# Sixteen experts' weights in tiles of whole rows, gate before up, and a moved combine and gather

## The chip, the cores and the metric

The kernel is one program on one core of one Trainium2 chip. It runs three transformer-like blocks over 512 tokens of 1024 channels, one after the other. The metric is the time on the device in microseconds (us). Three runs of the kernel before took 3489.10, 3494.49 and 3498.57 us; their median is 3494.49 us.

## The reference, cut to what matters

Only the mixture of experts at the end of the first block is touched by the change. There are 16 experts, and each takes the 64 tokens that score highest for it (capacity 2 * 512 / 16 = 64):

```
logits = h @ w_router;  aff = softmax(logits)            # h: 512 x 1024
top_w, top_idx = top_k(aff.T, 64)                        # 64 tokens for each of 16 experts
xe = h[top_idx]                                          # 16 x 64 x 1024
g  = xe @ w_gate[e];  u = xe @ w_up[e]                   # 1024 x 2048 each
y  = (silu(g) * u) @ w_down[e]                           # 2048 x 1024
out = zeros.at[top_idx].add(y * top_w)                   # back to the 512 tokens
```

All of it is float32. An expert has three matrices of 8.39 MB; the 16 experts have 402.7 MB, and every byte is read once from device memory.

## The kernel before, in words

`phase_m` holds the mixture of experts; `phase_a` runs before it, `phase_b` and `phase_c` (the other two blocks) after it. The experts are taken in pairs, p = 0 to 7, so that 2 x 64 tokens fill the 128 partitions.

For one pair the work has these parts. `gather(p)` (L2271) multiplies the tokens by a one-hot matrix on TensorE (L2277) and writes the pair's tokens `xe`, scaled and shifted, by ScalarE and VectorE (L2284, L2286). `expert(e, ...)` (L2318) does one expert. `weights(p)` (L2297) makes `gT`, which holds a token's weight for each slot; it multiplies on GpSimd (L2302) and transposes on TensorE (L2304). `combine(p, ...)` (L2357) multiplies the pair's results `yp` by `gT` (L2362) and adds them to the sums `acc` on VectorE (L2369).

In `expert`, the 2048 hidden columns are done in two halves, c = 0 and 1. Within a half, loads of gate and of up take turns: four tiles of each, and each tile holds two blocks of 128 rows by 1024 columns (`wexp`, L2309). A partition of a tile thus receives two separate pieces of 4096 bytes. Four matmuls use a tile, two for each block, whose outputs lie on the lower and the upper 64 partitions of one bank of PSUM (L2330). Then come silu on ScalarE (L2336), the product on VectorE (L2338) and four transposes (L2341) into `tp`, whose copy is `hTe`. After both halves eight tiles of down follow, 256 rows of 1024 columns each, again in two pieces of 4096 bytes to a partition, with four matmuls to a tile (L2352). Each expert therefore has 24 tiles of 1 MiB: eight of gate, eight of up, eight of down.

All weight loads are issued by SyncE (SP) in order, on one DMA queue. `wtile` (L284) hands out the room: the first 16 tiles have room of their own (12 in the rotation, four `wpre`); from then on a tile takes the room of the one 12 places before it, and its load waits until TensorE has used that. A tile's room may be called `w`, `wh` or `wx`; the names say nothing about the content.

The order on each engine is not the order of the Python text: a planner that works with estimated costs and priorities orders the whole program at build time, so that transposes, gather and combine can stand between the matmuls of an expert. `s.tc.issue_after(last.ins)` (L2332) only forces the last quarter of the first gather behind a given matmul.

In the text, `gather(p + 1)` and `weights(p)` stand between the two experts of a pair, and `combine(p)` stands after the second. The share of the last pair is added in `tiles()` (L2384), inside `phase_b`.

Of the kernel before, what the change touches and what calls it, by code (L numbers as in the profile page):

```python
# [19 lines left out]
P = 128  # L20
# [15 lines left out]
# name: (K, N, k tiles in a chunk, columns in a chunk)  # L36
# [33 lines left out]
# columns of a rotated head of 64 whose halves are 0..31 and 32..63, so that partners lie 16 apart  # L70
# [3 lines left out]
def _pair_cols(n_kv, rep):  # L74
    # heads (2g, r), (2g+1, r) side by side
    out = []
    for g in range(n_kv // 2):
        for r in range(rep):
            for s in range(2):
                h = (2 * g + s) * rep + r  # L80
                out.append(np.arange(64) + 64 * h)
    return np.concatenate(out)


def _tables_2d(n_meta):
    """cos and signed sin of the 2-d rotation, channel p of a head on partition p (64 twice)."""
# [12 lines left out]
def host(i):  # L99
    """Inputs of the program: layouts of the given arrays, and constants of the shapes."""  # L100
# [70 lines left out]
def _rwkv_masks():  # L171
    """[row in chunk (twice), direction, masks of 64 columns]: s before t; s up to t; for blocks of 1 to 32
    the diagonal and the rows of the later half of a pair against the columns of the earlier; the first of
    these transposed."""
# [38 lines left out]
class Kern:  # L213
# [24 lines left out]
    def a8(s, name, w=512):  # L238
        """Eight channel tiles."""
        q = [s.a4(f"{name}{i}", w) for i in range(2)]  # L240
        return [q[k // 4][:, k % 4] for k in range(8)]

    def parts(s, name, w=512):
        """Room for the two parts of eight channel tiles."""
# [9 lines left out]
    def split(s, x, h, l, scale=None):  # L254
        """x (times scale) as the sum of two float32r tiles h and l."""
# [9 lines left out]
    def stack(s, t, out, pr):  # L265
        """out: the parts of head pr of a pair of heads, h at the head's own rows, l at the other's."""
# [5 lines left out]
    def swap(s, a, b):  # L272
        """b: the halves of stack's a in the other order. a's product with a stack of another, plus b's, is exact."""
        for h in range(2):
            s.nc.gpsimd.dma_start(b[64 * h:64 * h + 64].bitcast(F32R), a[64 - 64 * h:128 - 64 * h].bitcast(F32R))

    def wsplit(s, name, ci, ki=0, into=None):
        """A chunk of weights as two float32r tiles whose sum it is."""
# [28 lines left out]
    def consts(s):  # L307
# [16 lines left out]
        # for a norm that follows another: the products of the gains, the squares of the first's  # L324
# [22 lines left out]
    def ssq(s, st, c0, tiles, nt, scale=None, first=True, last=True, ntok=P, add=None):  # L347
        """Column c0+n of st[tokens]: the sum over channels of squares of token tile n."""
# [5 lines left out]
    def sumsq(s, st, c0, x, nt, k, kt, first=True, last=True, ntok=P, add=None, **kw):  # L354
        """One of kt tiles of ssq: all but the last are first added up."""
# [15 lines left out]
    def twonorms(s, x, gains, xh, xl, lin, lead):  # L371
        """For a norm followed by a second one: the parts of x times both's gains, tile by tile, each followed by
        lead(k, parts); a psum tile whose columns 0..3 get the tokens' sums of squares of x, 4..7 those of x times
        the first norm's gains."""
# [24 lines left out]
    def factors(s, st, pool):  # L399
        """The tokens' factors of the first norm, 1 / sqrt(m), and of both, 1 / sqrt(m2 + eps m), of twonorms' sums."""  # L400
# [14 lines left out]
    def spread(s, r, nt, out, psum):  # L415
        """out[:, 128 n + t] = r[t, n] on every partition."""
# [10 lines left out]
    def lin(s, name, j, kt, x, ps, w=None, ntile=512):  # L427
        """ps = (x @ W[:, 128 j : 128 j + 128]).T of channel-major x."""
# [3 lines left out]
    def wcols(s, name, j0, nj):  # L432
        """Yields j, f for column tiles j0..j0+nj-1; f(k) is the k-th stationary tile."""
# [12 lines left out]
    def wcols3(s, name, j0, nj):  # L446
        """As wcols; f(k) is the pair of parts of the k-th stationary tile."""
# [10 lines left out]
    def cols(s, gen, x, lin):  # L458
        """Yields j, its product for the column tiles of wcols3."""
# [5 lines left out]
    def mm3(s, ps, a, b, first, last):  # L465
        """ps (+)= a.T @ b of pairs of parts."""
# [8 lines left out]
    def turns(*gens):  # L475
        """Takes the generators' stages by turns."""
# [10 lines left out]
    def heads_spread(s, r, n, psum):  # L487
        """psum[64 h + i, t] = r[t, h] for n tokens: r is [tokens, 2]."""
# [8 lines left out]
def phase_b(s, x2):  # L497
    nc, d = s.nc, s.d
    T2 = 528
    with ExitStack() as octx:  # L500
# [18 lines left out]
        # the meta tokens' keys, each head's among zeros, and the queries' scores against them  # L519
# [3 lines left out]
        # the meta tokens' keys, rates and running sums as a chunk padded with zeros  # L523
# [17 lines left out]
        # the meta tokens  # L541
# [75 lines left out]
        def normrot(t, W, g, out, sc):  # L617
            """Norm over each head's 64 channels, then rotation; W = 528 with the meta tokens first."""
# [93 lines left out]
        def load(n):  # L712
            """Loads of the recurrence's step n."""
# [38 lines left out]
def rwkv_prep(s, p1, lin, lin2, r4, k4, v4, wd, ad, bd2, bo_d, ch_d, v_d, mt):  # L752
    """Rates, keys and running sums of the decays' logarithms, by chunk in DRAM; the bonus."""
# [20 lines left out]
    # token-major v by chunk, the meta tokens last  # L774
# [12 lines left out]
    for t in range(4):  # L787
# [31 lines left out]
        # kk is kept negated  # L819
# [4 lines left out]
        # bonus  # L824
# [17 lines left out]
# direction, chunk, chunk of v: the meta tokens precede the forward chunks  # L842
# [3 lines left out]
def rwkv(s, ps, pr_, load, srcs, v_d, msk, y4, fill):  # L846
    """The recurrences over chunks of 64 tokens, both directions by turns. Two chunks are prepared at a time, stage
    by stage in turn with the chain of the chunk before them and a piece of fill."""
# [5 lines left out]
    # buffers, some of them in the room of the weights  # L854
# [30 lines left out]
    def prep(n):  # L885
# [44 lines left out]
        # N + I, then the inverse of I - N.T by doubling the blocks  # L930
# [107 lines left out]
def attn_b(s, ps, p3, qT, kT, vt, sm, mxm, yb_d):  # L1038
    """Yields after each stage of a pair of heads of a block of queries."""
# [4 lines left out]
    # the parts of the other keys, one above the other, in either order  # L1044
# [57 lines left out]
def branch_b(s, ps, yb_d, ga_d, yb, mg):  # L1102
    """The first half of the attention branch's columns. Yields after each stage."""
# [20 lines left out]
def tail_b(s, pb, y4, gd_d, bd2, bo_d, yb, mg, ga_d, xr_d):  # L1124
    nc, d = s.nc, s.d
    with ExitStack() as ctx:
# [14 lines left out]
        def branch(br, wn, y, j0):  # L1141
            """Yields after each column tile."""
# [86 lines left out]
def rot_tables(s, pool, ang):  # L1229
    """cos and signed sin of the positions' angles, to DRAM."""  # L1230
# [29 lines left out]
def phase_c(s, x, out):  # L1260
    nc, d = s.nc, s.d
    with ExitStack() as octx:
# [89 lines left out]
        with ExitStack() as ctx:  # L1352
# [29 lines left out]
            # the block before ends with a norm that this layer's follows  # L1382
# [19 lines left out]
            def state(n):  # L1402
                """The sums over the tokens of blocks up to n."""
# [33 lines left out]
            def norm(h, g, sq):  # L1437
                """The head's factors spread, times its gated output."""
# [311 lines left out]
def phase_a(s):  # L1750
    nc, d = s.nc, s.d
    with ExitStack() as ctx:
# [57 lines left out]
        # v_a's first columns are taken along as the tiles of h come  # L1810
# [79 lines left out]
        # v_a, token-major, normed; its gains and biases follow the mix  # L1890
# [25 lines left out]
        # the context's modulated norm  # L1916
# [10 lines left out]
        # u_a, spatial mix  # L1927
# [53 lines left out]
        # gates and merge  # L1981
# [22 lines left out]
        # k, v of the context and of the tokens  # L2004
# [411 lines left out]
```

## Time and profile before

| | |
|---|---|
| median of three runs | 3494.49 us |
| lowest, highest run | 3489.10, 3498.57 us |
| the profiled execution, span from first to last instruction | 3488.8 us |
| TensorE, busy share of the span | 93% |
| DMA read from device memory | 629.26 MB |
| queue of the weights (q1), packets and bytes | 183440, 614.38 MB |

No time of its own beside its span is recorded for the profiled execution; its span lies 5.7 us below the median of the runs. Stretches are given in us from the start of the span. A busy TensorE in a table is not a TensorE at its peak: matmuls are pipelined and their ends are modelled. A DMA "share" is the mean share of the 16 DMA engines that were busy; it can pass 1 because packets overlap. The matmul in float32 is two instructions in the trace, so the four matmuls of a tile show as x8.

### The profile page before, as it was taken

The numbers are of one execution on the slowest core, as the hardware profiler recorded it, in microseconds if no ns is written. First come the engines' busy times: TensorE is split into PE (matmuls) and PEld (weight loads), VectorE is DVE, ScalarE is ACT, GpSimd is POOL, SyncE is SP. The second block draws the span as 40 slices with busy tenths as digits, with TensorE's granted clock in tenths as the row PEclk, the third lists the DMA queues.
The fourth block names the chain that finished last, engine by engine and source line by source line (L and its number), as shares of the span: only waits on it lengthen the run. The fifth ranks groups of instructions, "written<-read, shape, count | busy, mean of one in ns | idle before, by whom it ended". The sixth has DMA issues, their size and how long they took to land.

```text
span 3488.8 us, 50427 instructions
## 1 busy us (share of the span) xinstructions
PE 3246.9 (93%) x21039; PEld 2255.2 (65%) x21039; DVE 1642.5 (47%) x3051; ACT 880.8 (25%) x1513; POOL 466.3 (13%) x531
## 2 busy tenths in 40 slices
PE   5999999898898898888999999999999999999998
PEld 4888778432332233224976777778877887888876
DVE  7658874311011011014666777763234665443674
ACT  2334552100000000002123433333233312222332
POOL 4202001000000000002022222203310111212201
PEclk9999999899999999999999999999999999999999
DMA  6564114999999999995335211142222231223211
GB/s 255 200 217 130 46 65 163 347 404 409 409 409 409 409 409 409 409 409 212 128 123 158 51 46 42 55 157 97 87 93 86 101 108 49 97 97 121 100 49 49
DMA packets 209060, 663.93 MB, mean 190 GB/s; under 512 B 55056, under 2 KB 66336, under 8 KB 186176
## 3 DMA queue, kind: packets, MB, share of 16 engines
q1 hardware_dynamic: 183440, 614.38, 47.0%
q10 hardware_dynamic: 21088, 35.70, 3.0%
q0 software_dynamic: 4304, 10.63, 1.0%
q8 instruction: 165, 2.70, 0.3%
q14 instruction: 63, 0.52, 0.0%
HBM read 629.26 MB, written 29.29 MB: 189 GB/s over the span
## 4 chain that ended last, share of the span: by engine, by line
PE 75%; DMA 15%; DVE 6%; issue 2%; ACT 1%; POOL 1%; SPq 0%; DVEq 0%; POOLq 0%; ACTq 0%
PE lin L468 39%; PE acc L468 5%; DMA wx_w_up_e<-in_w_up_e_dram 4%; PE up L2330 4%; PE bank L881 4%; DMA wh_w_up_e<-in_w_up_e_dram 4%; DMA wx_w_down_e<-in_w_down_e_dram 4%; PE gp L2330 3%; DMA wx_w_gate_e<-in_w_gate_e_dram 3%; PE mm L2277 2%; PE mm L2362 2%; PE y L2352 2%; PE lin L2144 1%; PE bank L921 1%; PE ch L881 1%
## 5 line engine op out<-in xcount | busy, mean ns | idle before, releaser
L2338 DVE TENSOR_TENSOR hm<-sl,up 128x512 f32<-128x512 f32 x32 | 22.0, 688 | 446.4 <-PE up L2330 446.3
L2330 PE MATMUL up<-wx_w_up_e,xe 128*64 128x512 f32 x624 | 155.1, 598 | 21.2 <-DMA wx_w_up_e<-in_w_up_e_dram 21.2
L468 PE MATMUL lin<-xh,wl_ev_in 128*128 128x512 f32 x384 | 155.8, 406 | 0.0
L468 PE MATMUL lin<-uh,wl_w_in 128*128 128x264 f32 (+1 forms) x448 | 150.4, 338 | 2.5 <-DVE rs_y L343 1.2
L468 PE MATMUL lin<-xl,wh_ev_in 128*128 128x512 f32 x384 | 151.4, 394 | 0.0
L468 PE MATMUL lin<-xh,wh_ev_in 128*128 128x512 f32 x384 | 151.3, 394 | 0.0
L468 PE MATMUL lin<-ul,wh_w_in 128*128 128x264 f32 (+1 forms) x448 | 146.6, 328 | 3.4 <-DVE ul L262 3.4
L259 DVE TENSOR_TENSOR wl_w_ff<-w_w_ff,wh_w_ff 128x2048 fp32r<-128x2048 f32 x32 | 73.3, 2292 | 154.5 <-ACT wh_w_ff L258 154.5
L468 PE MATMUL lin<-uh,wh_w_in 128*128 128x264 f32 (+1 forms) x448 | 145.9, 327 | 0.0
L2336 ACT ACTIVATE sl<-gp 128x512 f32<-128x512 f32 x32 | 19.1, 597 | 486.9 <-PE gp L2330 479.6
L2330 PE MATMUL gp<-wx_w_gate_e,xe 128*64 128x512 f32 x496 | 124.5, 600 | 15.6 <-DMA wx_w_gate_e<-in_w_gate_e_dram 15.5
L2352 PE MATMUL y<-wh_w_down_e,hTe 128*64 128x512 f32 x512 | 119.8, 599 | 20.0 <-DMA wh_w_down_e<-in_w_down_e_dram 19.9
L2302 POOL TENSOR_TENSOR gw<-oh,aff 128x128 f32<-128x128 f32 x32 | 12.8, 401 | 898.0 <-PE mm L2362 585.3
L304 DVE COPY yp<-y 64x512 f32<-64x512 f32 x16 | 11.0, 688 | 241.7 <-PE y L2352 124.1
L2330 PEld LDWEIGHTS up<-wx_w_up_e,xe 128*64 128x64 f32 x624 | 43.3, 136 | 121.0 <-issue 69.0
L258 ACT CAST wh_w_in<-w_w_in 128x2048 fp32r<-128x2048 f32 x39 | 74.4, 1906 | 155.0 <-PE lin L468 135.7
L468 PE MATMUL lin<-hh,wl_w_in 128*128 128x512 f32 x272 | 111.9, 411 | 0.7 <-DVE t L1886 0.6
L468 PE MATMUL lin<-hh,wh_w_in 128*128 128x512 f32 x272 | 108.3, 398 | 0.0
L468 PE MATMUL lin<-hl,wh_w_in 128*128 128x512 f32 x272 | 108.3, 398 | 0.0
L259 DVE TENSOR_TENSOR wl_w_in<-w_w_in,wh_w_in 128x2048 fp32r<-128x2048 f32 x39 | 90.1, 2310 | 38.5 <-ACT wh_w_in L258 38.3
L468 PE MATMUL acc<-fl,wh_w_ff 128*128 128x512 f32 x256 | 103.3, 404 | 1.4 <-DVE fl L259 1.4
L468 PE MATMUL acc<-fh,wl_w_ff 128*128 128x512 f32 x256 | 100.2, 397 | 4.2 <-ACT fh L258 4.2
(870 smaller groups left out, 8262.6 us busy)
## 6 DMA issues: line engine op xcount, KB each, us to landing
wx_w_up_e<-in_w_up_e_dram SPq DMA_DIRECT2D x78, 1024.0 KB, 18.6
wh_w_down_e<-in_w_down_e_dram SPq DMA_DIRECT2D x64, 1024.0 KB, 18.8
wx_w_gate_e<-in_w_gate_e_dram SPq DMA_DIRECT2D x62, 1024.0 KB, 18.5
w_w_down_e<-in_w_down_e_dram SPq DMA_DIRECT2D x48, 1024.0 KB, 18.5
w_w_in<-in_w_in_dram SPq DMA_DIRECT2D x39, 1024.0 KB, 4.9
w_w_gate_e<-in_w_gate_e_dram SPq DMA_DIRECT2D x32, 1024.0 KB, 18.8
wh_w_up_e<-in_w_up_e_dram SPq DMA_DIRECT2D x32, 1024.0 KB, 18.2
wh_w_gate_e<-in_w_gate_e_dram SPq DMA_DIRECT2D x32, 1024.0 KB, 18.3
```

Source lines behind the costliest of these rows:

```text
L258: s.nc.scalar.copy(h, x)
L259: s.nc.vector.tensor_tensor(l, x, h.bitcast(F32), op=OP.subtract)
L468: s.nc.tensor.matmul(ps, x, y, start=first and i == 0, stop=last and i == 2)
L881: nc.tensor.matmul(ps_[q, t], lhs(t, h, q), rhs(t, h, q), start=True, stop=True)
L921: nc.tensor.matmul(S[:, t, :w_ar], KD[:, t].rearrange("p a s -> p (a s)"), AR[h][:, t, :w_ar], start=True, stop=True)
L2144: nc.tensor.matmul(pv[64 * pr:64 * pr + 64, rr * P:(rr + 1) * P], vt[:, 64 * g:64 * g + 64], pt[:, (2 * i + pr) * P:(2 * i + pr + 1) * P], ...
L2277: nc.tensor.matmul(t[:, k % 4 * P:k % 4 * P + P], ht[n][k // 4][:, k % 4 * P:k % 4 * P + P], oh[n][p // 4][:, 2 * (p % 4):2 * (p % 4) + 2] ...
L2330: last = nc.tensor.matmul(o[64 * j:64 * j + 64], xe[:, k, 64 * e2:64 * e2 + 64], w[:, k2, 512 * j:512 * j + 512], start=k == 0, stop=k == 7)
L2336: nc.scalar.activation(sl, gp, AF.Silu)
L2338: nc.vector.tensor_tensor(hm, sl, up, op=OP.mult)
L2352: nc.tensor.matmul(y[64 * jj:64 * jj + 64], hT[c][:, i, 64 * j:64 * j + 64], w[:, f2, 512 * jj:512 * jj + 512], start=f == 0, stop=f == 15)
L2362: nc.tensor.matmul(t, yp[:, k * P:(k + 1) * P], gT, start=True, stop=True)
```

## The change

The weights come in other tiles. A tile of gate or up is now 128 whole rows of 2048 columns, and a tile of down is 128 pairs of neighbouring rows. Either way a partition receives one piece of 8192 bytes, and the whole tile is one run of 1 MiB in device memory. The number of tiles, their size, the order of SP's loads within down, and the room are as before.

An expert now sums gate over all eight tiles into two banks of PSUM, then up over all eight tiles into two others. Silu follows gate, and the product follows up; then `between()` is called, and only then come the eight transposes. `between` is `combine` of the pair before in the first expert of a pair, and `gather(p + 1)` and `weights(p)` in the second. The transposes read `hm` with a step of two columns, to match the pairs of rows in down. `turn` is given its PSUM tile instead of a tag. The rest of the diff sets `gT` to None ahead of the loop and removes comments.

```diff
-        def turn(i, tag, bufs):
-            t = ps.tile([P, 512], F32, tag=tag, bufs=bufs, name=tag)
+        def turn(i, t):
...
+        pair = lambda tag: ps.tile([P, 2, 512], F32, tag=tag, name=tag)
+        one = lambda tag: ps.tile([P, 512], F32, tag=tag, name=tag)
+        gt0, ut0 = pair("g"), pair("u")
...
-        def wexp(name, e, r0, c0):
+        def wexp(name, e, i):
             w = d[name]
-            K, N = w.shape[1], w.shape[2]
             t = s.wtile(name)
-            v = t[:].rearrange("p (k c) -> p k c", k=2)
-            nc.sync.dma_start(v, bass.AP(tensor=w.tensor, offset=w.offset + e * K * N + r0 * N + c0,
-                                         ap=[[N, P], [P * N, 2], [1, 1024]]))
-            return v
+            nc.sync.dma_start(t, bass.AP(tensor=w.tensor, offset=w.offset + (8 * e + i) * 2048 * P, ap=[[2048, P], [1, 2048]]))
+            return t
...
+        def expert(e, xe, yp, rest=(), between=lambda: None):
+            es = slice(64 * (e % 2), 64 * (e % 2) + 64)
+            def wide(tag, name, rest=()):
+                o = pair(tag)
+                for k in range(8):
+                    w = wexp(name, e, k)
+                    for j in range(4):
+                        last = nc.tensor.matmul(o[64 * (j % 2):64 * (j % 2) + 64, j // 2], xe[:, k, es],
+                                                w[:, 512 * j:512 * j + 512], start=k == 0, stop=k == 7)
+                    if k == 1:
+                        with s.tc.issue_after(last.ins):
+                            for _ in rest:
+                                pass
+                return o
+            gp = wide("g", "w_gate_e", rest)
+            hm = []
+            for b in range(2):
+                hm.append(s.a("hm"))
+                nc.scalar.activation(hm[b], gp[:, b], AF.Silu)
+            up = wide("u", "w_up_e")
+            for b in range(2):
+                nc.vector.tensor_tensor(hm[b], hm[b], up[:, b], op=OP.mult)
+            between()
             hT = []
+            for b in range(2):
+                t = one("tp")
+                v = hm[b].rearrange("p (q c x) -> p q x c", q=2, x=2)
+                for q in range(2):
+                    for x in range(2):
+                        nc.tensor.transpose(t[:, (2 * q + x) * P:(2 * q + x + 1) * P], v[:, q, x], s.ident)
+                h = s.a("hTe", 4, P)
+                s.copy(h, t[:].rearrange("p (i c) -> p i c", i=4))
+                hT.append(h)
+            y = one("y")
+            for f in range(8):
+                w = wexp("w_down_e", e, f)
+                b, h, q = f // 4, f // 2 % 2, f % 2
+                for x in range(2):
+                    for j in range(2):
+                        nc.tensor.matmul(y[64 * j:64 * j + 64], hT[b][:, 2 * q + x, 64 * h:64 * h + 64],
+                                         w[:, 1024 * x + 512 * j:1024 * x + 512 * j + 512], start=f + x == 0, stop=f + x == 8)
...
-            expert(2 * p, xe, yp, rest)
-            nxt = list(gather(p + 1))[0] if p < 7 else None
-            gT = weights(p)
-            expert(2 * p + 1, xe, yp)
-            if p < 7:
-                combine(p, yp, gT)
-            xe = nxt
+            expert(2 * p, xe, yp, rest, lambda: old and combine(*old))
+            def ahead():
+                nonlocal xe, gT
+                if p < 7:
+                    xe = list(gather(p + 1))[0]
+                gT = weights(p)
+            expert(2 * p + 1, xe, yp, (), ahead)
+            old = p, yp, gT
```

## Rows read from the trace of the kernel before

**Rows 1.** The page, 40 slices of 87.2 us: busy tenths of the DMA engines; GB/s

```profile
DMA  6564114999999999995335211142222231223211
GB/s 255 200 217 130 46 65 163 347 404 409 409 409 409 409 409 409 409 409 212 128 123 158 51 46 42 55 157 97 87 93 86 101 108 49 97 97 121 100 49 49
```

**Rows 2.** The chain of waits at the stage's end: start us, us, what

```profile
1561.64 1.96 PE up L2330 x8
...
1563.92 18.15 DMA wx_w_up_e<-in_w_up_e_dram
...
1584.71 18.00 DMA wx_w_down_e<-in_w_down_e_dram
...
1602.76 1.96 PE y L2352 x8
```

**Rows 3.** Windows: stretch, us, PE, PEld, DVE, ACT, POOL busy, PEclk, DMA share, GB/s

```profile
12.00:30.00 18.00, 3.94 (x10) 2.28 (x10) 16.07 (x20) 4.33 (x4) 8.25 (x4) 1.00 1.01 423
619.90:638.00 18.10, 3.25 (x24) 2.60 (x22) 15.58 (x34) 3.74 (x8) 0.00 (x0) 0.69 1.00 372
645.00:699.40 54.40, 53.56 (x285) 23.94 (x284) 4.50 (x9) 5.77 (x10) 1.20 (x3) 1.00 0.95 358
699.40:752.60 53.20, 51.53 (x217) 17.32 (x216) 6.34 (x10) 5.22 (x10) 0.00 (x0) 1.00 1.02 401
752.60:1602.70 850.10, 737.76 (x3301) 247.32 (x3300) 90.32 (x148) 47.70 (x92) 11.23 (x28) 1.00 1.03 409
```

**Rows 4.** TensorE in order of time, late: start, us, tile, count [idle before <-releaser]

```profile
1543.73 1.94 PE L2330 MATMUL gp<-wx_w_gate_e,xe 128*64 128x512 f32 x8 [0.62 <-DMA wx_w_gate_e<-in_w_gate_e_dram]
1546.30 1.94 PE L2330 MATMUL up<-wx_w_up_e,xe 128*64 128x512 f32 x8 [0.63 <-DMA wx_w_up_e<-in_w_up_e_dram]
1548.86 1.94 PE L2330 MATMUL gp<-wx_w_gate_e,xe 128*64 128x512 f32 x8 [0.62 <-DMA wx_w_gate_e<-in_w_gate_e_dram]
```

**Rows 5.** DMA queues in 12 to 30 us and in 1400 to 1500 us

```profile
DMA packets 1074, 7.62 MB, mean 423 GB/s; under 512 B 129, under 2 KB 145, under 8 KB 145
...
DMA packets 10602, 40.92 MB, mean 409 GB/s; under 512 B 623, under 2 KB 623, under 8 KB 10598
```

**Rows 6.** TensorE in order of time, the first pair of experts

```profile
644.94 1.94 PE L2330 MATMUL gp<-w_w_gate_e,xe 128*64 128x512 f32 x8
...
677.19 0.66 PE L2341 MATMUL tp<-ident,hm 128*128 128x128 f32 x4 [0.84 <-DVE hm L2338]
...
691.66 7.41 PE L2277 MATMUL mm<-oh,ht 128*128 128x128 f32 x64
698.90 0.60 PE L2304 MATMUL mm<-ident,gw 128*128 128x128 f32 x4
...
701.20 1.89 PE L2330 MATMUL up<-wx_w_up_e,xe 128*64 128x512 f32 x8
702.92 1.89 PE L2330 MATMUL gp<-wx_w_gate_e,xe 128*64 128x512 f32 x8
...
744.97 7.71 PE L2362 MATMUL mm<-gT,yp 128*128 128x512 f32 x16 [0.79 <-DVE yp L304]
752.61 1.94 PE L2330 MATMUL gp<-wx_w_gate_e,xe 128*64 128x512 f32 x8
```

**Rows 7.** TensorE's waits, 752.6 to 1602.7 us: us in total, times, longest

```profile
PE up L2330 <- DMA wx_w_up_e<-in_w_up_e_dram: 21.2, 34, 0.6
...
PE tp L2341 <- DVE hm L2338: 19.2, 22, 0.9
...
PE up L2330 <- DMA w_w_up_e<-in_w_up_e_dram: 4.1, 7, 0.6
```

**Rows 8.** SP's queue in order of time: two weight loads

```profile
669.51 0.37 SPq L2314 DMA_DIRECT2D wx_w_up_e<-in_w_up_e_dram  x1
679.74 0.37 SPq L2314 DMA_DIRECT2D w_w_gate_e<-in_w_gate_e_dram  x1
```

**Rows 9.** Groups of instructions, 645 to 1605 us: count | busy us, mean ns | idle

```profile
L304 ACT COPY hTe<-tp 128x512 f32<-128x512 f32 x16 | 9.4, 586 | 47.9 <-PE tp L2341 47.9
```

More of the change, by code (lines that the diff above doesn't have):

```diff
@@ L2220, in turn @@
             return t
-        turned = [turn(i, *b) for i, b in enumerate((("g", 2), ("g", 2), ("u", 2), ("u", 2), ("tp", 1), ("y", 1)))]
+        pair = lambda tag: ps.tile([P, 2, 512], F32, tag=tag, name=tag)
+        one = lambda tag: ps.tile([P, 512], F32, tag=tag, name=tag)
+        gt0, ut0 = pair("g"), pair("u")
+        turned = [turn(i, t) for i, t in enumerate((gt0[:, 0], gt0[:, 1], ut0[:, 0], ut0[:, 1], one("tp"), one("y")))]
         r = pm.tile([P, 4], F32, name="r")
@@ L2243, in phase_m @@
             if i >= 6:
-                turned.append(turn(i, "mm", 2))
+                turned.append(turn(i, mm()))
             nc.scalar.activation(ht[i // 2][i % 2], turned[i], AF.Copy, scale=r[:, i // 2:i // 2 + 1])
@@ L2268, in phase_m @@
                                         pos[:, n, 8 * q + e.start:8 * q + e.stop, None].to_broadcast([P, w, 64]), op=OP.is_equal)
-        acc = []
+        acc, gT = [], None
         def gather(p):
@@ L2307, in weights @@
             return gT
-        def wexp(name, e, r0, c0):
+        def wexp(name, e, i):
             w = d[name]
-            K, N = w.shape[1], w.shape[2]
             t = s.wtile(name)
-            v = t[:].rearrange("p (k c) -> p k c", k=2)
-            nc.sync.dma_start(v, bass.AP(tensor=w.tensor, offset=w.offset + e * K * N + r0 * N + c0,
-                                         ap=[[N, P], [P * N, 2], [1, 1024]]))
-            return v
-        def expert(e, xe, yp, rest=()):
-            e2 = e % 2
-            hT = []
-            for c in range(2):
-                gp = ps.tile([P, 512], F32, tag="g", bufs=2, name="gp")
-                up = ps.tile([P, 512], F32, tag="u", bufs=2, name="up")
-                for kk in range(4):
-                    for o, nm in ((gp, "w_gate_e"), (up, "w_up_e")):
-                        w = wexp(nm, e, kk * 256, c * 1024)
-                        for k2 in range(2):
-                            k = 2 * kk + k2
-                            for j in range(2):
-                                last = nc.tensor.matmul(o[64 * j:64 * j + 64], xe[:, k, 64 * e2:64 * e2 + 64],
-                                                        w[:, k2, 512 * j:512 * j + 512], start=k == 0, stop=k == 7)
-                    with s.tc.issue_after(last.ins):
-                        for _ in rest:
-                            pass
-                sl = s.a("sl")
-                nc.scalar.activation(sl, gp, AF.Silu)
-                hm = s.a("hm")
-                nc.vector.tensor_tensor(hm, sl, up, op=OP.mult)
-                t = ps.tile([P, 512], F32, tag="tp", name="tp")
-                for i in range(4):
-                    nc.tensor.transpose(t[:, i * P:(i + 1) * P], hm[:, i * P:(i + 1) * P], s.ident)
-                ht_ = s.a("hTe", 4, P)
-                s.copy(ht_, t[:].rearrange("p (i c) -> p i c", i=4))
-                hT.append(ht_)
-            y = ps.tile([P, 512], F32, tag="y", name="y")
-            for ff in range(8):
-                w = wexp("w_down_e", e, ff * 256, 0)
-                for f2 in range(2):
-                    f = 2 * ff + f2
-                    c, j, i = f // 8, (f // 4) % 2, f % 4
-                    for jj in range(2):
-                        nc.tensor.matmul(y[64 * jj:64 * jj + 64], hT[c][:, i, 64 * j:64 * j + 64],
-                                         w[:, f2, 512 * jj:512 * jj + 512], start=f == 0, stop=f == 15)
-            for jj in range(2):
-                s.copy(yp[64 * e2:64 * e2 + 64, 512 * jj:512 * jj + 512], y[64 * jj:64 * jj + 64])
@@ new lines, in wexp @@
+            nc.sync.dma_start(t, bass.AP(tensor=w.tensor, offset=w.offset + (8 * e + i) * 2048 * P, ap=[[2048, P], [1, 2048]]))
[23 more added lines that the diff above has]
+            between()
+            hT = []
+            for b in range(2):
[15 more added lines that the diff above has]
+                                         w[:, 1024 * x + 512 * j:1024 * x + 512 * j + 512], start=f + x == 0, stop=f + x == 8)
+            for j in range(2):
+                s.copy(yp[es, 512 * j:512 * j + 512], y[64 * j:64 * j + 64])
@@ L2372, in phase_m @@
         xe = next(rest)
+        old = ()
         for p in range(8):
             yp = s.a4("yp").rearrange("p t w -> p (t w)")[:, :1024]
-            expert(2 * p, xe, yp, rest)
-            nxt = list(gather(p + 1))[0] if p < 7 else None
-            gT = weights(p)
-            expert(2 * p + 1, xe, yp)
-            if p < 7:
-                combine(p, yp, gT)
-            xe = nxt
+            expert(2 * p, xe, yp, rest, lambda: old and combine(*old))
[6 more added lines that the diff above has]
+            old = p, yp, gT
         s.wx = None
```

## The prediction

> **What bounds the kernel now.** I read the page's slices first, to see which stage the change touches and what is at its limit there [rows 1]. Slices 9 to 18, some 700 to 1570 us, show the DMA engines full at a level 409 GB/s, slice after slice; that is the experts' stage, and no other stage looks like it. The chain of waits shows the same from the end backwards [rows 2]: a load of 18 us, one tile's matmuls, the next load of 18 us, down to the last tile of down at 1602.76 us. So the stage ends when the last weights have come, and TensorE adds one tile's work.
>
> Next I read TensorE's own rows, to see how much room it has. In the late part a tile starts every 2.56 us (1546.30 - 1543.73, 1548.86 - 1546.30), and each tile waits for its load [rows 4]. Where tiles are there already, one takes 1.72 us (702.92 - 701.20) [rows 6]. The waits from 752.6 us on come to 88.0 us for weights, the sum of nine lines between 21.2 and 4.1 us, and to 19.2 us for the product `hm` ahead of the transposes [rows 7].
>
> Only the beginning differs. From 645 to 699.4 us TensorE is busy for 53.56 of 54.40 us and the DMA moves 358 GB/s; to 752.6 us it is 401 GB/s; from there 409 GB/s [rows 3]. At first the loads wait for TensorE to give room back: SP issues tile 27 at 669.51 us and tile 28 only at 679.74 us, when the first tile of down has been used [rows 8]. Later TensorE waits for the loads.
>
> **The change part by part.** *The piece of a load.* 402.7 MB come in the same 384 tiles, but each partition gets one piece of 8192 bytes in place of two of 4096. The trace before shows both sizes with the DMA engines full. From 1400 to 1500 us the pieces are of 4096 bytes: 10602 packets less 623 small ones make 40.87 MB, at 409 GB/s. From 12 to 30 us the first weights of the program come in pieces of 8192 bytes: 1074 packets less 145 smaller ones make 7.61 MB, at 423 GB/s [rows 5]. The same queue and the same tile of 1 MiB stand in both. I take 423 for the new tiles, since that row has the same shape of load.
>
> - From 752.6 us to the end: 850.1 us at 409 GB/s [rows 3] become 850.1 * 409 / 423 = 822.0 us, so -28.1 us. The ends are 0, if the rate stays at 409, and -28.1 - 2.0 = -30.1 us, if it is 424, a rounding above the row.
> - From 699.4 to 752.6 us: 401 GB/s, so the queue ran short for a little while. What moved there would take 53.2 * 401 / 409 = 52.2 us at full rate, and at 423 it takes 50.4: -1.7 us if the short spell stays as it is. Ends 0 and -2.8 (53.2 us from 401 to 423); I take -1.7.
> - From 645 to 699.4 us: no gain, since SP waits for TensorE there [rows 8].
>
> *Transposes at the end of up.* Before, the four of the first half stood among the second half's matmuls. Now all eight follow up, and `tp` has one bank: the second four wait for the copy of the first. An expert's TensorE thus has four transposes, 0.66 us [rows 6], and a copy, 0.586 us [rows 9], with about as much again for hand-overs, more in line: at most 1.9 us. In the first expert this holds back the first tile of down, whose room tile 28 needs [rows 6, 8]: 0 to +1.9 us on the end, and I take +1.0. In the other 15 the waits for weights hide it: of 88.0 us, 28 go with the faster loads, and 60 are left over 14 experts, 4.3 us each. If that cover were gone, 15 * 1.9 = 28 us would be due, just the gain.
>
> *Gate first, then up.* The 16 tiles come in another order, with the same four matmuls each; gate's silu falls beside up's matmuls. Nothing on the path: 0. The four outputs in two banks need no more time by anything in the rows; TensorE has 88 us to spare.
>
> *Combine and gather moved.* Their instructions stay the same in number: 64 and 4 on TensorE for gather and weights (7.41 + 0.60 us), 16 for combine (7.71 us) [rows 6]. They issue no DMA, and SP's order of loads is unchanged but for gate and up, so nothing new stands ahead of a load. Before, they stood between experts; now between up and the transposes. That adds a wait in three places. On TensorE, transposes and down stand behind them: a stop of 7.7 to 8.0 us in which no room is given back. Such a stop already stands in the trace, 8 us at 691.66 and 7.7 us at 744.97 [rows 6], and over the whole late part, with all these stops in it, the DMA keeps 409 GB/s [rows 3]. On VectorE, `hTe`'s copies stand behind eight additions, but TensorE reaches its transposes only after combine as well. On GpSimd, the four products `gw` have to be ready; the planner may put them early. In return the wait for `hm`, 0.84 us ahead of the transposes [rows 6], is filled by that work, up to -19.2 us of TensorE's time in all [rows 7]. None of it is on the path: 0, as long as TensorE needs less for a pair than the loads. It needs 752.61 - 644.94 = 107.7 us for the first pair, where it hardly waits [rows 6]; 48 tiles at 423 GB/s take 48 * 1.0486 / 0.423 = 119.0 us. The room is 11 us for a pair; what is late next is still the load.
>
> *The tail.* After the last tile of down come four matmuls, the copies of `y` and the last pair's share, as before: 0.
>
> The sum: -28.1 - 1.7 + 1.0 = -28.8 us. Against the profiled execution, 3488.8 us become 3460.0. The runs' median, 3494.49, lies 5.7 us above that span; I leave that distance as it is and get 3465.7, rounded to **3465 us**.
>
> **A rule of the Trainium skill, weighed.** By the rows, a byte in pieces of 8192 costs 3.3% less time than in pieces of 4096 (409 / 423) [rows 5]. The Trainium skill, "DMA: Bandwidth & Descriptors", section "Why small descriptors are slow (HBM only)", gives a fixed cost of about 3 cycles for a packet beside one cycle for each 32 bytes; my estimate from that is 2 * 131 cycles against 259, 1.1% less. The sum by it would be about -9.8 us in place of -28.1 for the long stretch; the trace shows three times that step, and the measurement decides.
>
> **The rivals.**
>
> *Half the step.* The 18 us at the start differ in more than the piece: TensorE is busy for 3.94 of 18 us there and almost always later [rows 3]. If half of the step from 409 to 423 comes from that, the rate is 416, and 850.1 * 409 / 416 gives -14.3 us: 3480 us. For it: one short row. Against: in the late part, too, the rate keeps to one level whatever TensorE does.
>
> *No step.* The device memory or the way into SBUF gives 409 GB/s in this stage, whatever the piece, or the load of 8192 bytes is cut in two again: 3494 us. For it: the level line of 409. Against: 423 on the same queue. The same page of the Trainium skill, section "Where 436 GB/s comes from", speaks for this rival, as it says that loads from device memory are bound at about 358 GB/s by the memory; the trace, at 409 and 423, does not agree.
>
> *Slower: TensorE becomes the bound.* After the stop behind up, the granted clock falls to the lower level, 1.2 GHz, and the eight tiles of down take 27.4 us in place of 8 * 1.72 = 13.7. A pair then needs 107.7 + 27.4 = 135.1 us, against 48 * 2.564 = 123.1 us at 409 GB/s. Seven pairs with 12.0 us too many make +84 us: 3578 us. It decides from the point at which a pair's TensorE time passes 123.1 us, 15.4 above what I read. For it: the clock's mean is 0.69 between 619.9 and 638 us, where TensorE worked for 3.25 of 18.1 us. Against: it is 1.00 in all three later stretches [rows 3], in spite of 88 us of waits, and the new stop is filled with matmuls.
>
> **How the numbers follow.** The forecast has a chance of 0.79: large, since the stage is bound by one resource and the trace has the new load's rate. Half the step gets 0.07, no step 0.09, the slower case 0.03, and 0.02 is left for a plan of the later stages that comes out worse by more than 10 us, since the planner orders the whole program anew. The forecast's own range is 3456 to 3474: 30.1 + 2.8 us of gain give 3461.6 and a scatter of the runs of 5 us (their spread is 9.5) goes below it; +1.9 and a rate of 420 go above. To hold 8 in 10 with a part of the second case I take 3453 to 3482. A difference under about 0.3%, 10.5 us, can't be told from none in this kernel. Faster by more than that: the forecast and half the step, 0.86; within it: no step and a part of the rest, 0.10; slower: 0.04.
>
> **What would show it.** Right: from the second pair on, windows at 421 to 424 GB/s in place of 409; tiles of the late part 2.47 to 2.49 us apart, each still waiting for its load; packets of the weight queue halved; the last tile of down some 29 us earlier; from there to the end of the span the same 1886 us. The waits for `hm` gone or small, and no stretch in which SP waits for room while DMA engines idle, except before 700 us. Wrong: 409 GB/s with 8192-byte pieces (no step); a rate of 423 with gaps, or TensorE without waits for weights (TensorE is the bound); a clock under 1.00 after 700 us; or an end of the stage at 1574 us with a total that does not follow it (the later stages changed).

## The result, and the profile after

The changed kernel takes 3465.98 us, median of 4 runs (3463.98 to 3470.01); the kernel before, beside it on the same chip, 3496.53 us (4 runs, 3489.10 to 3498.97). The ratio is 0.9921, with a 95% interval of 0.9909 to 0.9933: 23 to 32 us less. 3465 was forecast.

The slices of the page, 86.6 us each, busy tenths of the DMA engines and GB/s:

```profile
DMA  6554114899999999994335211142222321233211
GB/s 248 200 215 141 47 54 171 324 421 420 420 421 421 420 420 421 420 421 174 117 129 152 52 42 37 55 169 87 98 85 95 115 86 52 95 109 114 96 49 49
```

The shelf of 409 GB/s [rows 1] now stands at 420 to 421, and the ninth slice, which stood at 404, is at full height too. The stage is still the loads' stage; they have become faster.

The windows, with the columns of [rows 3] (stretch, us, busy time of PE, PEld, DVE, ACT, POOL, granted clock, DMA share, GB/s):

```profile
12.00:30.00 18.00, 3.94 (x10) 2.28 (x10) 16.15 (x20) 4.28 (x3) 8.19 (x4) 1.00 1.02 423
622.40:640.50 18.10, 3.09 (x23) 2.24 (x21) 15.55 (x34) 3.77 (x8) 0.00 (x0) 0.69 1.01 423
648.90:701.90 53.00, 53.00 (x265) 20.59 (x266) 3.60 (x7) 4.45 (x7) 1.20 (x3) 1.00 0.92 372
701.90:752.60 50.70, 48.27 (x237) 19.60 (x234) 4.99 (x9) 4.69 (x10) 0.00 (x0) 1.00 1.01 420
752.60:1578.50 825.90, 743.99 (x3304) 257.46 (x3302) 91.81 (x151) 47.10 (x95) 11.54 (x28) 0.99 1.01 420
```

The first row is the stretch from which I took the new rate, again at 423. The second is the first load of experts' weights, 372 GB/s before and 423 now, with TensorE doing as little as then. Most of that step is not the piece: before, the rate was 334 GB/s up to 629 us and 411 from there to 638, and the new order with the old tiles (experiment 2) has 405 from 619.9 to 638 us. What slowed the first half of that load is open. The last row is the long stretch: 420, where I forecast 423.

The DMA queues between 1000 and 1100 us:

```profile
DMA packets 5777, 42.08 MB, mean 421 GB/s; under 512 B 644, under 2 KB 644, under 8 KB 644
```

Nothing lies between 2 and 8 KB any more; [rows 5] have nearly all packets there. Over the program the weight queue sends 134288 packets instead of 183440: 49152 fewer, which is 384 tiles of 128 pieces.

TensorE in order of time, late (start us, us, what, count, and in brackets the idle time ahead of it and what ended that):

```profile
1520.67 1.94 PE L2327 MATMUL g<-wx_w_gate_e,xe 128*64 128x512 f32 x8 [0.54 <-DMA wx_w_gate_e<-in_w_gate_e_dram]
1523.16 1.94 PE L2327 MATMUL g<-wx_w_gate_e,xe 128*64 128x512 f32 x8 [0.55 <-DMA wx_w_gate_e<-in_w_gate_e_dram]
1525.66 1.94 PE L2327 MATMUL g<-wx_w_gate_e,xe 128*64 128x512 f32 x8 [0.57 <-DMA wx_w_gate_e<-in_w_gate_e_dram]
...
1561.27 0.75 PE L2351 MATMUL tp<-ident,hm 128*128 128x128 f32 x4 [0.86 <-DVE hm L2343]
1562.75 0.74 PE L2351 MATMUL tp<-ident,hm 128*128 128x128 f32 x4 [0.73 <-ACT hTe L304]
1563.43 5.37 PE L2361 MATMUL y<-w_w_down_e,hTe 128*64 128x512 f32 x24
...
1578.55 1.94 PE L2361 MATMUL y<-wx_w_down_e,hTe 128*64 128x512 f32 x8 [0.55 <-DMA wx_w_down_e<-in_w_down_e_dram]
1581.89 0.20 PE L546 MATMUL lin<-ones,msq 128*16 128x1 f32 x2 [1.41 <-DVE yp L304]
```

A tile comes every 2.49 us (2.56 in [rows 4]) and still waits for its load. The two groups of four transposes wait 0.86 us for `hm` and 0.73 us for the copy between them; the three tiles of down that came meanwhile then go through without a wait (5.37 us), so the delay is caught up.

The row of line 546 is the first of the stage that follows. Before, it starts at 1606.10 us and the experts' first gate matmuls at 644.94 [rows 6], 961.2 us apart; now 1581.89 and 648.85, 933.0 us apart: **28.1 us in this stage**. After it the program takes 1883.2 us (1882.7 before). In this execution the stage started 3.9 us later, so the spans differ by 3488.8 - 3465.1 = 23.7 us. That start lies between 644.9 and 649.3 us in the nine profiled executions of this study, and before's is the earliest of them; what moves it was not followed up.

### The profile page after: what moved, and what is told of

Its sections match the earlier page's. It is cut to its first block, busy times and chain, and to the rows that moved or that the text cites. A ratio compares the mean times of both kernels' runs of the same rounds, so it can differ in the third digit from the quotient of the medians.

```text
span 3465.1 us, 50408 instructions
## 1 busy us (share of the span) xinstructions
PE 3252.8 (94%) x21039; PEld 2267.3 (65%) x21039; DVE 1642.0 (47%) x3051; ACT 878.1 (25%) x1513; POOL 461.8 (13%) x531
## 3 DMA queue, kind: packets, MB, share of 16 engines
q1 hardware_dynamic: 134288, 614.38, 45.9%
## 4 chain that ended last, share of the span: by engine, by line
PE 74%; DMA 15%; DVE 6%; issue 2%; ACT 1%; POOL 1%; SPq 0%; POOLq 0%; DVEq 0%; ACTq 0%
PE lin L468 39%; DMA wx_w_down_e<-in_w_down_e_dram 6%; PE acc L468 5%; DMA wh_w_gate_e<-in_w_gate_e_dram 4%; DMA wx_w_up_e<-in_w_up_e_dram 4%; PE bank L881 4%; PE g L2327 4%; PE u L2327 3%; PE y L2361 2%; PE mm L2279 2%; PE mm L2371 1%; PE lin L2144 1%; PE bank L921 1%; PE ch L881 1%; PE lin L2131 1%
## 5 line engine op out<-in xcount | busy, mean ns | idle before, releaser
L2327 PE MATMUL u<-wx_w_up_e,xe 128*64 128x512 f32 x632 | 145.1, 598 | 20.5 <-DMA wx_w_up_e<-in_w_up_e_dram 20.5
L2343 DVE TENSOR_TENSOR hm<-hm,u 128x512 f32<-128x512 f32 x32 | 20.6, 683 | 277.6 <-PE u L2327 277.6
L2327 PEld LDWEIGHTS u<-wx_w_up_e,xe 128*64 128x64 f32 x632 | 42.1, 136 | 120.7 <-issue 69.3
L2327 PE MATMUL g<-wx_w_gate_e,xe 128*64 128x512 f32 x488 | 113.3, 599 | 2.2 <-DMA wx_w_gate_e<-in_w_gate_e_dram 2.2
L468 PE MATMUL acc<-fh,wh_w_ff 128*128 128x512 f32 x256 | 101.9, 398 | 0.0
```

Of the source, the lines that this page charges most:

```text
L468: s.nc.tensor.matmul(ps, x, y, start=first and i == 0, stop=last and i == 2)
L2327: last = nc.tensor.matmul(o[64 * (j % 2):64 * (j % 2) + 64, j // 2], xe[:, k, es], w[:, 512 * j:512 * j + 512], start=k == 0, stop=k == 7)
L2343: nc.vector.tensor_tensor(hm[b], hm[b], up[:, b], op=OP.mult)
```

## The experiments

**Theory.** All of the gain is the piece of a load: 8192 bytes in place of 4096, at the same number of bytes. **Rivals.** That the tile now lies in one run of memory; that part of the step from 409 to 423 GB/s is TensorE's idleness (half the step); that the order of gate, up, combine and gather has a share.

**1. The loads by themselves.** Everything else is left out; groups of 40 MiB, each with another shape of load, twelve tiles of 1 MiB in flight.

```diff
-        phase_c(s, phase_b(s, phase_m(s, phase_a(s))), out)
+    # 4096: parts of rows 8192 apart; parts of one run
+    group("g4s", G, 2048, 12, [(two, ..., [[2048, P], [2048 * P, 2], [1, 1024]]) ...])
+    group("d4c", D, 2048, 12, [(two, i * M, [[1024, P], [1024 * P, 2], [1, 1024]]) ...])
+    # 8192: one run; rows 16384 apart
+    group("g8c", G, 2048, 12, [(None, (N + i) * M, [[2048, P], [1, 2048]]) ...])
+    group("d8s", D, 2048, 12, [(None, ..., [[4096, P], [1, 2048]]) ...])
+    # 2048; 16384 in 2 MiB tiles; 32768 in 4 MiB tiles; 8192 in 2 MiB tiles
...
```

> Everything but loads of experts' weights is left out; eight groups of 40 MiB are loaded one after the other with nothing else running, which differ in the piece that a partition gets and in whether a tile is one run of device memory. Theory 'piece' (a fixed cost for each piece, 10.5 ns by 160.2 ns for 4096 bytes at 409 GB/s and 309.9 ns for 8192 at 423): 2048 bytes 384 GB/s, 4096 bytes 409 whether strided or one run, 8192 bytes 423 whether strided or one run and also in tiles of 2 MiB, 16384 bytes 430, 32768 bytes 434. Rival 'one run' (what counts is that a tile is one run of 1 MiB): 4096 bytes in one run 423, 8192 bytes with rows apart 409. Rival 'half the step' (TensorE's work costs the other half): 4096 bytes 416 or more with TensorE idle.

The windows of that kernel, a stretch from the middle of each group in the order 4096 in parts of rows, 4096 in one run, 8192 in one run, 8192 in parts of rows, 2048, 16384, 32768, 8192 in 2 MiB tiles (columns: stretch, us, DVE, POOL, clock, DMA share, GB/s):

```profile
10.00:98.00 88.00, 0.00 (x0) 0.00 (x0) 1.00 1.03 410
112.00:200.00 88.00, 0.00 (x0) 0.00 (x0) 1.00 1.03 410
220.00:310.00 90.00, 0.00 (x0) 0.00 (x0) 1.00 1.01 422
322.00:405.00 83.00, 0.00 (x0) 0.00 (x0) 1.00 1.01 423
425.00:515.00 90.00, 0.00 (x0) 0.00 (x0) 1.00 1.05 387
535.00:615.00 80.00, 0.00 (x0) 0.00 (x0) 1.00 1.01 429
635.00:715.00 80.00, 0.00 (x0) 0.00 (x0) 1.00 1.00 432
735.00:815.00 80.00, 0.00 (x0) 0.00 (x0) 1.00 1.01 422
```

The rate goes by the piece. One run or parts of rows: 410 and 410, 422 and 423. A DMA of 2 MiB in pieces of 8192: 422, as with 1 MiB. And with TensorE silent pieces of 4096 still give 410, so its work is not what held the old pieces at 409. One of 16 engines needs 16 * 2048 / 387 = 84.7 ns for a piece of 2048 bytes, 159.8 ns for 4096, 310.6 for 8192, 611 for 16384, 1214 for 32768. Two pieces of half the size take 9.5, 9.1, 10.1 and 8.5 ns more than one (the rates are rounded to whole GB/s, which leaves the third open by 1.5 ns and the last by 3): **each piece costs some 9 to 10 ns beside its bytes**, at every size as far as these rates tell.

**2. Each part of the change alone.** The new tiles with the old order (gate and up by turns, combine and gather in their old place; the eight transposes stay behind up):

```diff
-            gp = wide("g", "w_gate_e", rest)
+            gp, up = pair("g"), pair("u")
+            for k in range(8):
+                for o, nm in ((gp, "w_gate_e"), (up, "w_up_e")):
+                    w = wexp(nm, e, k)
...
-            expert(2 * p, xe, yp, rest, lambda: old and combine(*old))
...
+            expert(2 * p, xe, yp, rest)
+            nxt = list(gather(p + 1))[0] if p < 7 else None
+            gT = weights(p)
+            expert(2 * p + 1, xe, yp)
+            if p < 7:
+                combine(p, yp, gT)
```

> The new tiles alone: gate and up take turns tile by tile, combine and gather stand where they stood before. Theory 'piece': 420 GB/s in the stage, the whole gain, -28 us against before (3469 us), the same as the changed kernel within 4 us. Rival 'order' (gate first and the moves give the gain): 0 to -8 us, 3489 us or more.

3466.74 us, ratio 0.9921 (0.9908 to 0.9935): the whole gain.

The changed kernel with only combine and gather back in their old place (the last lines of that diff alone):

> The changed kernel with combine and gather back in their old places in the text. Theory 'piece': the moves are beside the path, the same as the changed kernel within 4 us (-28 us against before). Rival 'order': a part of the gain is lost, -20 us or less.

3465.09 us, ratio 0.9912 (0.9899 to 0.9926): the whole gain again.

The new order with the old tiles:

```diff
-        def wexp(name, e, i):
+        def wexp(name, e, r0, c0):
...
+            nc.sync.dma_start(v, bass.AP(..., ap=[[N, P], [P * N, 2], [1, 1024]]))
...
+                for kk in range(4):
+                    for c in range(2):
+                        w = wexp(name, e, kk * 256, c * 1024)
```

> Gate first and the moves, but the old tiles with two pieces of 4096 bytes. Theory 'piece': 409 GB/s, the same as before within 4 us (3496 us). Rival 'order': -20 us or more.

3491.48 us beside 3495.09 of before, ratio 0.9991 (0.9983 to 1.0): between nothing and 6 us.

Windows over the first 54 us of the stage, the next 54 and the rest, columns as above, first of the new order with old tiles:

```profile
646.30:700.30 54.00, 54.00 (x269) 20.81 (x270) 3.68 (x7) 4.45 (x7) 1.20 (x3) 1.00 0.95 355
700.30:754.30 54.00, 51.57 (x248) 20.18 (x246) 5.69 (x10) 5.74 (x11) 0.00 (x0) 1.00 1.03 409
754.30:1602.50 848.20, 741.93 (x3290) 249.30 (x3286) 91.18 (x150) 46.07 (x93) 11.53 (x28) 1.00 1.03 409
```

and of the new tiles in the old order:

```profile
647.60:701.60 54.00, 54.00 (x293) 24.61 (x294) 5.17 (x11) 6.76 (x12) 0.40 (x1) 1.00 0.91 371
701.60:755.60 54.00, 51.50 (x222) 17.67 (x220) 5.56 (x9) 4.59 (x8) 1.20 (x3) 1.00 1.01 414
755.60:1578.80 823.20, 741.73 (x3292) 258.19 (x3288) 89.30 (x148) 45.55 (x91) 9.96 (x25) 0.99 1.01 420
```

The last rows settle the main question: the long stretch goes by the tile alone, 409 with the old and 420 with the new, under either order. The middle rows show the one small thing that the order does: there the old order runs short of its own level (401 of 409 before [rows 3], 414 of 420 here), the new order does not (409 of 409 here, 420 in the changed kernel).

**3. The dose the other way.** Pieces of 2048: four parts of 512 columns in a tile, two tiles used by turns.

```diff
-            nc.sync.dma_start(t, bass.AP(..., ap=[[2048, P], [1, 2048]]))
+            nc.sync.dma_start(v, bass.AP(..., ap=[[N, P], [P * N, 4], [1, 512]]))
...
+                        w = [wexp(name, e, kk * 512, c * 1024 + 512 * j) for j in range(2)]
```

> The changed kernel with four pieces of 2048 bytes to a partition in place of one of 8192 (two tiles at a time, so that the matmuls still take both halves of the columns by turns). Theory 'piece': the rate of 387 GB/s measured for loads alone, some 385 in the stage; 850.1 us at 409 become 850.1 * 409 / 385 = 903 us, +53 us against before: 3548 us, within 8. Rival 'one run' (it only matters whether a tile is one run of memory): the same as before, 3495 us.

3542.42 us beside 3494.12, ratio 1.0139 (1.0125 to 1.0153): slower by 48 us. Its window from 1000 to 1500 us, columns as above:

```profile
1000.00:1500.00 500.00, 435.18 (x1860) 157.96 (x1859) 49.28 (x79) 25.72 (x49) 6.41 (x16) 1.00 1.05 387
```

387 GB/s, the loads' own rate with such pieces.

**4. Combine and gather held behind up.** In the changed kernel the planner did not put them between up and the transposes. TensorE there, in the first pair of experts:

```profile
731.36 0.75 PE L2351 MATMUL tp<-ident,hm 128*128 128x128 f32 x4 [0.79 <-DVE hm L2343]
732.96 0.75 PE L2351 MATMUL tp<-ident,hm 128*128 128x128 f32 x4 [0.85 <-DVE hTe L304]
733.64 5.37 PE L2361 MATMUL y<-w_w_down_e,hTe 128*64 128x512 f32 x24
...
748.38 1.12 PE L2371 MATMUL mm<-gT,yp 128*128 128x512 f32 x2 [0.79 <-DVE yp L304]
749.43 1.94 PE L2327 MATMUL g<-wx_w_gate_e,xe 128*64 128x512 f32 x8
751.30 1.98 PE L2371 MATMUL mm<-gT,yp 128*128 128x512 f32 x4
```

Combine (`mm<-gT,yp`) stands in small groups among the next expert's gate tiles, in place of one stop of 7.7 us as in [rows 6]; the transposes have nothing ahead of them and wait. So I made it stand where the code has it:

```diff
-            up = wide("u", "w_up_e")
+            up, last = wide("u", "w_up_e")
...
-            between()
+            with s.tc.issue_after(last.ins):
+                between()
```

> The changed kernel with the matmuls of combine, gather and weights held behind the last matmul of up, where the text puts them and the planner did not. Theory 'piece, TensorE has room': the same as the changed kernel within 4 us (3466 us), 420 GB/s. Rival 'the stop starves the loads': gaps in the DMA engines after each stop, 10 us or more above the changed kernel.

3467.80 us, ratio 0.9927 (0.9913 to 0.9941). TensorE in order of time in that kernel:

```profile
896.64 1.94 PE L2327 MATMUL u<-wx_w_up_e,xe 128*64 128x512 f32 x8 [0.56 <-DMA wx_w_up_e<-in_w_up_e_dram]
898.51 1.98 PE L2372 MATMUL mm<-gT,yp 128*128 128x512 f32 x4
900.33 0.63 PE L2352 MATMUL tp<-ident,hm 128*128 128x128 f32 x4
900.80 5.69 PE L2372 MATMUL mm<-gT,yp 128*128 128x512 f32 x12
906.33 0.63 PE L2352 MATMUL tp<-ident,hm 128*128 128x128 f32 x4
906.89 5.37 PE L2362 MATMUL y<-w_w_down_e,hTe 128*64 128x512 f32 x24
...
926.50 1.94 PE L2327 MATMUL g<-wx_w_gate_e,xe 128*64 128x512 f32 x8 [0.50 <-DMA wx_w_gate_e<-in_w_gate_e_dram]
```

At this place the waits for `hm` and for the copy are filled, as I had thought of it, and the tiles that came meanwhile are worked off at 1.72 us each until at 926.50 TensorE waits for a load again. From 752.6 to 1578.5 us the waits for `hm` come to 0.3 us; those for the copy are not gone, 9.6 us in 8 waits of up to 3.2. From 760 to 1500 us the DMA keeps 420 to 421 GB/s. Where this work stands does not set the time.

**5. A larger piece.** The same mechanism asks for more: 16384 bytes. Two thirds of the weights (those tiles for which the room allows it) come in tiles of 2 MiB. In the control such a tile still has two pieces of 8192 for each partition; in the other kernel the weights lie in the program's inputs so that two blocks' rows follow each other, and it has one of 16384. In both kernels the 16384 bytes stand side by side in the partition; only their places in device memory differ.

```diff
 control:
+            t = s.wp.tile([P, 4096], F32, tag="wh", bufs=2, name="wh_" + name)
+            nc.sync.dma_start(t..., bass.AP(..., ap=[[2048, P], [2048 * P, 2], [1, 2048]]))
 pieces of 16384, against the control:
-    o["w_gate_e"] = f["w_exp_gate"][0]
+    o["w_gate_e"] = np.ascontiguousarray(f["w_exp_gate"][0].reshape(16, 4, 2, P, 2048).transpose(0, 1, 3, 2, 4))
...
+            nc.sync.dma_start(t, bass.AP(tensor=w.tensor, offset=off, ap=[[4096, P], [1, 4096]]))
```

> The changed kernel with two thirds of the weights in tiles of 2 MiB (two pieces of 8192 bytes to a partition) and the room rearranged for them: the control for the next. Theory 'piece': the same as the changed kernel within 4 us (3466 us). Rival 'coarse tiles': room comes back later, 5 us or more above it.

> As the one before, but the host lays the experts' weights out so that these tiles give a partition one piece of 16384 bytes. Theory 'piece': 429 against 422 GB/s for loads alone, 2.444 against 2.482 us for a MiB; two thirds of some 340 tiles after the start save 8.7 us against the control, 3457 us. Rival 'nothing above 8192': the same as the control.

The control takes 3464.84 us, ratio 0.9919 (0.9906 to 0.9933): the larger DMA gives nothing by itself. With pieces of 16384 it is 3458.83 us (3456.90 to 3460.37), ratio 0.9902 (0.9888 to 0.9915): 6.0 us below its control, whose slowest and fastest run lie 1.2 us apart, and the fastest of all kernels here. Windows from 1000 to 1500 us, the control:

```profile
1000.00:1500.00 500.00, 441.56 (x2005) 163.70 (x2005) 56.47 (x90) 27.60 (x52) 6.42 (x16) 0.98 1.01 421
```

and pieces of 16384, with the DMA queues from 1000 to 1100 us:

```profile
1000.00:1500.00 500.00, 444.56 (x2027) 164.68 (x2027) 58.45 (x93) 28.20 (x53) 7.22 (x18) 0.98 1.01 425
...
DMA packets 3872, 42.54 MB, mean 425 GB/s; under 512 B 430, under 2 KB 430, under 8 KB 430
```

**All kernels by one measure**: from the first gate matmul to line 546's row (line 539 in the two kernels with tiles of 2 MiB), in the profiled executions.

| kernel | piece, bytes | order | starts, us | ends, us | stage, us |
|---|---|---|---|---|---|
| pieces of 2048 | 2048 | new | 647.00 | 1661.12 | 1014.1 |
| before | 4096 | old | 644.94 | 1606.10 | 961.2 |
| new order, old tiles | 4096 | new | 646.32 | 1606.50 | 960.2 |
| new tiles, old order | 8192 | old | 647.61 | 1582.82 | 935.2 |
| combine and gather back | 8192 | half | 647.03 | 1581.35 | 934.3 |
| control of 2 MiB | 8192 | new | 649.29 | 1583.94 | 934.7 |
| held behind up | 8192 | new | 648.50 | 1581.75 | 933.3 |
| after | 8192 | new | 648.85 | 1581.89 | 933.0 |
| pieces of 16384 | 16384 for 2/3 | new | 648.22 | 1575.09 | 926.9 |

Each doubling of the piece gives half of what the one ahead of it gave. Under the new order 2048 to 4096 gives 54 us (1014.1 to 960.2) and 4096 to 8192 gives 27 (to 933.0); half of that again is an estimate of 13.5 us for all weights, 9 for two thirds of them, and 8 were measured (934.7 to 926.9). That is what a fixed price for each piece does: from 4096 to 8192 an engine has 49152 / 16 = 3072 pieces fewer, and 27 us over them are 8.9 ns each.

## Why the prediction was right, step by step

**What bounds the stage: right.** The loads did before and do after; kernels whose pieces differ have another time, and those whose pieces are alike lie within some 5 us of each other.

**The piece, right in its mechanism.** Experiments 1 to 3 and 5 show it from both sides. The term was 28.1 us for the long stretch and nearly nothing for the beginning; the stage gained 28.1 us in all, but split otherwise. That the sum of 28.8 us lies so near is luck in part: the long stretch was taken 4.9 us too large, the two stretches ahead of it 2.4 us too small, and the 1.0 us for the transposes was not seen.

- *The long stretch* runs at 420 to 421 GB/s, not 423: 850.1 * (1 - 409 / 420.5) = 23.2 us, so this term was 4.9 us too large. My row for 423 was the right load, but 18 us of it, and it was luck that it read so: the same stretch reads 422 to 424 in five of the nine profiled executions and 404, 408, 410 and 413 in the other four, with the same loads. Loads alone, over 83 to 90 us, give 422 to 423 with these pieces and 410 with the old; with the kernel's work around them 420.5 and 409. So I had set a rate with little work beside it against one with all of it. The rival of half the step put a real effect there, but its size is 1 to 2 GB/s, not 7; which part of the work takes it was not tested.
- *From 645 to 699.4 us* I gave nothing, since SP waits for TensorE there. The rate went from 358 to 372 GB/s; over 53.0 us that is 53.0 * 14 / 420 = 1.8 us. Experiment 2 puts it down to the tile (371 with it in the old order, 355 without it). That transfers gain in a stretch in which the queue waits for room I had excluded wrongly. My reading, not shown, is that between the waits they run at the full rate, and that rate rose. The room counts for as much: the control of 2 MiB and the pieces of 16384, whose room is divided otherwise, have 357 and 355 over the same 54 us, so a larger piece gave nothing here.
- *From 699.4 to 752.6 us* I left the short spell as it was and gave 1.7 us; it is gone (420, where 401 stood), which makes 50.7 * 19 / 420 = 2.3 us.

These three are 27.3 us, within the rounding of the rates of the stage's 28.1.

**Transposes at the end of up: +1.0 us taken, nothing seen.** SP's queue in order of time, two weight loads (columns as in [rows 8], a row may hold several issues):

```profile
666.69 5.48 SPq L2315 DMA_DIRECT2D wx_w_gate_e<-in_w_gate_e_dram  x4
...
683.60 3.76 SPq L2315 DMA_DIRECT2D w_w_gate_e<-in_w_gate_e_dram  x3
```

Tile 28 is issued 34.75 us after the first gate matmul (683.60 - 648.85), against 34.80 (679.74 - 644.94) before. In this first expert the planner had put matmuls of gather ahead of and between the two groups of transposes. In the later ones TensorE catches up at once, as the late rows above show.

**Combine and gather: the price of 0 was right, the picture was wrong.** This is the step that failed. I wrote that their work would fill the wait for `hm`, "up to -19.2 us of TensorE's time", and that these waits would be gone or small. TensorE's waits from 752.6 to 1578.5 us (us in total, times, longest):

```profile
PE u L2327 <- DMA wx_w_up_e<-in_w_up_e_dram: 20.5, 35, 1.6
PE tp L2351 <- DVE hm L2343: 12.0, 14, 0.9
...
PE tp L2351 <- DVE hTe L304: 5.7, 7, 0.9
PE tp L2351 <- ACT hTe L304: 5.0, 7, 0.7
```

There is one wait for `hm` for each of 14 experts now, in place of 22 [rows 7], and a new one for the copy between the transposes: 12.0 + 10.7 = 22.7 us where 19.2 stood. The planner orders by its own costs, and the place in the code was only an offer to it. It costs nothing: 53.7 us of waits for weights are left (seven lines from 20.5 to 2.2; I had forecast 60), and experiment 4, with the waits for `hm` filled, is no faster.

**Gate first, and the moves: 0 in the forecast, 1 to 2 us in the traces.** The short spell in the second 54 us goes with the new order, and the stage is 1.0 us shorter with old tiles and 1 to 2 us with new ones (table above; one execution each, and the medians can't tell it apart).

**The start of the sum.** 5.7 us lay between the profiled execution of before and the median of its runs, and I carried them over. After, the profiled span (3465.1) lies 0.9 us below the median. The span that I forecast was 3460.0, so it came out 5.1 us too early: 3.9 us by the start of the stage, 0.7 by the stage and 0.5 by what follows. For the same reason the last tile of down, forecast some 29 us earlier, starts 24.2 us earlier (1578.55 against 1602.76). The two errors nearly cancel in 3465, which is luck; the stage's 28.1 us and the medians' 30.5 are what the mechanism can be held against.

**The rivals.** *No step* is ruled out by the 420 GB/s of the stage. *Half the step* is ruled out by the 410 GB/s of the old pieces without any work beside them. *Slower by the clock*: its mechanism came, its price did not. The granted clock is 0.99 in the long stretch, where 1.00 stood before, and anything under 1.00 was named as a sign of being wrong. In four of the 14 experts there it falls to 0.50, which is the level of 1.2 GHz, for some 3 to 4 us, each time behind the two waits at the transposes. One of the four:

```profile
1501.10 0.75 PE L2351 MATMUL tp<-ident,hm 128*128 128x128 f32 x4 [0.86 <-DVE hm L2343]
1502.63 0.91 PE L2351 MATMUL tp<-ident,hm 128*128 128x128 f32 x4 [0.79 <-DVE hTe L304]
1503.47 6.84 PE L2361 MATMUL y<-w_w_down_e,hTe 128*64 128x512 f32 x24
```

The clock is 0.50 from 1504 to 1506 us, and three tiles of down take 6.84 us here (6.76 to 7.00 in the four), where 5.37 stand without the fall. That is some 1.5 us a time, against the 13.7 us for every expert that the rival needs. TensorE still waits for weights, and the DMA keeps its rate, so it costs nothing.

**The rule weighed.** By pairs of sizes the loads alone show 410 / 387 = 1.059, 422 / 410 = 1.029 and 429 / 422 = 1.017. By the Trainium skill, "DMA: Bandwidth & Descriptors", section "Why small descriptors are slow (HBM only)", with 3 cycles a packet beside one for 32 bytes, my estimate is 1.023, 1.012 and 1.006. The form of the rule agrees, the fixed part is some two and a half to three times as large here.

## What to carry to other kernels

Where a stage runs at a level rate of loads and its engine waits for each of them, count the pieces, not the DMAs: this program's price is 9 to 10 ns for each piece on its DMA engine, so pieces per engine times that is what larger pieces can give, and each doubling gives half of the one ahead of it. Take both rates of the sum from stretches with the same work beside the loads. And where a planner orders the program, a place in the code is no place in time: look in the trace for where the work went before explaining anything by it.

## What the runs showed of the hardware

- The rate of one core's loads by the piece (loads alone): 387, 410, 422, 429 and 432 GB/s for 2048, 4096, 8192, 16384 and 32768 bytes. In the kernel too, with two thirds of the weights in pieces of 16384, that step still shows: 425 against 421 GB/s.
- How a tile lies in memory (one run, or parts of rows 8192 or 16384 bytes apart) made no difference beyond 1 GB/s, nor did DMAs of 2 MiB in place of 1 MiB.
- The whole kernel beside them takes at most 1 to 2 GB/s from a full stream of loads: 410 to 409, 422 to 420.5, and with pieces of 2048 nothing (387 both ways).
- Two waits of 0.7 to 0.9 us close together at the transposes were followed by a granted clock of 0.50 in 4 of 14 experts, and not in the other ten.
